# Down projection of a hybrid layer: sums of quarters stored by the gate and up stage, products summed over all pairs in PSUM

## The chip, the cores and the metric

The kernel runs on one core of one Trainium2 chip. The metric is the device time of one execution in microseconds (us). All engines of the core take part: TensorE (PE; PEld is its weight load), VectorE (DVE), ScalarE (ACT), GpSimd (POOL) and the queue of SyncE (SP), which issues nearly all transfers between DRAM and the on-chip memory SBUF. Matmul results are built in PSUM, which has eight banks of 128 x 512 float32.

## The reference

One layer: attention in two head groups, an output projection with a residual, and then the feed-forward part, which is what the change touches. There are 2048 tokens, the model width is 1024, the inner width `D_FF` is 2816, and all is float32.

```python
x = x + jnp.einsum('bse,ed->bsd', mixed, w_o[l])
h = rmsnorm(x, g_ffn[l])
act = jax.nn.silu(jnp.einsum('bsd,df->bsf', h, w_gate[l])) * jnp.einsum('bsd,df->bsf', h, w_up[l])
x = x + jnp.einsum('bsf,fd->bsd', act, w_down[l])
return rmsnorm(x, g_final)
```

## The kernel before

**Precision.** A float32 operand is split into a high part (ScalarE's rounding cast to fp32r) and a low part (the operand less the high part, a subtraction). A product then takes three matmuls: high x high, high x low and low x high. Such a split is therefore one ACT cast and one subtraction, on DVE or on POOL.

**Products of quarters.** Each large matrix product is done by the Strassen-Winograd scheme: both factors are cut into quarters, seven products of sums of quarters take the place of eight, and sums of the products give the result's quarters. In the names, A11, A12, A22 and S1 to S4 are a left quarter or a sum of left quarters; the products in the down projection are P1 to P7. P1 is A11 by its right quarter, P2 A12, P3 S4, P4 A22, P5 S1, P6 S2 and P7 S3, each by a quarter or a sum of quarters of `w_down`.

**Gate and up (`ffn_in`).** The tokens are taken in two halves (`t2`) of 1024. At the start of each half, `operands` loads the normalised input hT and makes the seven left operands with both parts, which stay in SBUF. Then come eleven pairs `j` of 128-wide blocks of the inner width. For each, `quads` runs the seven products with the gate weights (g) and then the seven with the up weights (u), 12 matmuls per product, in the PSUM banks X, Y and Z. `weights` loads the raw weights into a pool `rw` of four buffers (each 512 KB), forms their sums on DVE and splits them. `gated` applies the silu, and `upped` multiplies gate by up (L1094) and stores each of the four quarters of the activation to DRAM (L1097, 256 KB each). The first pair of each half uses `first_quads`, with one bank per product.

**Down (`ffn_out`).** Here the left factor is the activation, the right `w_down`. Each half of the tokens goes through three groups of pairs (4, 4 and 3); within a group the seven products follow in the order P1, P6, P2, P7, P5, P4, P3. A class `Pair` loads a pair's activation and weight quarters into two tiles E and F, and its method `operands` makes, product by product, the sums (L1154 to L1166) in place and the split (`split`: cast L1147, subtraction L1148) into a tile `o4` from a pool of six. The sums and part of the subtractions go to POOL: `alt` is POOL for odd pairs. A product's 12 matmuls per pair are at L1254. The PSUM banks are three sets of four (X, Y and Z, of which two can be in use at once), and after each group every product is evicted: `evict` adds it to the residual x1 held in SBUF (L1205), P1 goes to a tile `a1` (L1201, L1199), which is later added to three quarters (L1212). After the last group `square`, `finish` and the scalings L1192 apply the final normalisation and L1193 stores the result. The last two products of all are run together, one quarter of the tokens after the other.

**Order.** The order of the instructions on each engine is set when the program is built, from the order of the code and the pools' buffers. An engine works through its instructions in that order and waits on semaphores. SP's transfers do the same; each of them also waits for the eighth before it to have landed.

## Time and profile before

| | before |
|---|---|
| time, median of 3 runs | 2446.41 us (2442.75 to 2448.05) |
| the profiled execution, its own time | 2443.37 us |
| its span | 2441.6 us (1.8 us lie around it) |
| busy in the span: PE, DVE, ACT, POOL | 2312.3, 1702.8, 1054.3, 531.5 us |
| mean granted TensorE clock | 0.983 |
| gate and up, first half of the tokens | 1096 to 1526 us |
| gate and up, second half | 1526 to 1964 us |
| down projection | 1964 to 2441.6 us |
| moved by SP's queue in the span | 349.20 MB |

A row of the profile names the line, the engine, the operation, the tile written and the tiles read. A group of rows gives how many there are, their busy time in us, the mean of one in ns, and then the time that the engine stood idle just ahead of them with what ended it ("<-"). In a timeline the idle time and what ended it stand in brackets.

### The profile page before, as it was taken

How to read it: one execution, taken by the hardware profiler on the slowest of the kernel's cores; microseconds unless marked ns; L12 is line 12 of the kernel's file. 1: busy time of each engine (PE TensorE's matmuls, PEld its weight loads, DVE VectorE, ACT ScalarE, POOL GpSimd, SP SyncE). 2: the span in 40 equal slices, each digit the busy share in tenths (PEclk: the TensorE clock that was granted, in tenths of full speed). 3: DMA queues.
4: the chain of work that ended last, by engine and by line, in shares of the span. 5: the costliest groups of instructions: out<-in, count | busy, mean ns of one | idle time of the engine just before them, and what ended most of it. 6: DMA issues, size and time to landing. Idle time of an engine off the chain costs nothing.

```text
span 2441.6 us, 33440 instructions
## 1 busy us (share of the span) xinstructions
PE 2312.3 (95%) x11765; PEld 1949.7 (80%) x11765; DVE 1702.8 (70%) x3239; ACT 1054.3 (43%) x2371; POOL 531.5 (22%) x417
## 2 busy tenths in 40 slices
PE   7999999997999889998999999899999989998997
PEld 7987788886999777776888888688888868876885
DVE  5335554447999877659566665965556468999899
ACT  5323355554898843335333323432333233343333
POOL 2211211111111011113110111311011064345532
PEclk9999999998999999999999999999999999998999
DMA  7656666569987877744222222422222254334221
GB/s 219 213 181 215 166 180 179 151 157 241 230 217 196 230 214 201 249 180 145 82 86 91 78 87 74 138 83 87 77 90 84 100 220 138 138 104 139 102 87 69
DMA packets 245975, 361.17 MB, mean 148 GB/s; under 512 B 19872, under 2 KB 148512, under 8 KB 240304
## 3 DMA queue, kind: packets, MB, share of 16 engines
q1 hardware_dynamic: 242032, 349.20, 47.5%
q0 software_dynamic: 3488, 9.51, 1.3%
q8 instruction: 93, 1.52, 0.3%
q14 instruction: 74, 0.61, 0.1%
q10 hardware_dynamic: 288, 0.33, 0.0%
HBM read 240.36 MB, written 118.62 MB: 147 GB/s over the span
## 4 chain that ended last, share of the span: by engine, by line
PE 43%; DVE 10%; issue 3%; DMA 3%; POOL 2%; ACT 1%; SPq 0%; DVEq 0%; POOLq 0%; ACTq 0%
PE Yu L1022 7%; PE Yg L1022 7%; PE Zu L1022 5%; PE Xu L1022 5%; PE Zg L1022 4%; PE Xg L1022 4%; PE bY L1254 3%; PE acco L885 3%; DVE o L1148 3%; PE bZ L1254 2%; PE bX L1254 1%; DVE xo L1205 1%; DVE xo L1192 1%; DMA E<-in_w_down_dram 1%; DVE F L1161 1%
## 5 line engine op out<-in xcount | busy, mean ns | idle before, releaser
L1094 POOL TENSOR_TENSOR c<-c,c 128x512 f32<-128x512 f32 x66 | 103.2, 1566 | 664.9 <-DVE c L1040 311.6
L987 ACT CAST wh<-T 128x512 fp32r<-128x512 f32 x176 | 108.5, 622 | 252.4 <-PE Yg L1022 76.1
L1254 PE MATMUL bY<-o 128*128 128x512 f32 x792 | 195.5, 403 | 20.8 <-DVE o L1148 9.4
L468 DVE TENSOR_TENSOR hl<-pt,hl 128x512 fp32r<-128x512 f32 (+1 forms) x224 | 145.8, 658 | 80.9 <-ACT hl L467 80.4
L1254 PEld LDWEIGHTS bY<-o 128*128 128x128 f32 x792 | 152.6, 195 | 60.7 <-DVE o L1148 11.9
L443 ACT ACTIVATE p<-t,m 128x256 f32<-128x256 f32 (+1 forms) x384 | 177.4, 480 | 17.8 <-DVE m L668 17.8
L169 PE MATMUL acc<-hh,wh 128*128 128x512 f32 x416 | 170.2, 409 | 0.7 <-DVE vt L239 0.7
L169 PE MATMUL acc<-hh,wl 128*128 128x512 f32 x416 | 170.4, 410 | 0.0
L169 PE MATMUL acc<-hl,wh 128*128 128x512 f32 x416 | 170.1, 409 | 0.0
L885 PE MATMUL acco<-woh,oT 128*128 128x512 f32 x512 | 163.9, 398 | 4.4 <-ACT oT L856 3.4
L486 PE MATMUL o<-hl,v 128*128 128x128 f32 (+1 forms) x816 | 141.9, 294 | 7.5 <-DVE hl L468 6.8
L467 ACT CAST hl<-pt 128x512 fp32r<-128x512 f32 (+1 forms) x224 | 125.1, 568 | 45.3 <-PE pt L462 45.1
L421 PE MATMUL s<-k,q 128*128 128x256 f32 (+1 forms) x768 | 122.1, 290 | 18.2 <-DMA k<-kB 8.5
L462 PE MATMUL pt<-ident,p 128*128 128x128 f32 x848 | 134.3, 280 | 4.1 <-DVE hl L468 1.8
L989 DVE TENSOR_TENSOR wl<-T,wh 128x512 fp32r<-128x512 f32 x176 | 124.5, 712 | 17.0 <-ACT wh L987 16.7
L1254 PE MATMUL bX<-o 128*128 128x512 f32 x528 | 125.4, 393 | 6.7 <-DVE o L1148 4.0
L1254 PEld LDWEIGHTS bX<-o 128*128 128x128 f32 x528 | 98.7, 189 | 31.5 <-DVE o L1148 6.8
L1254 PE MATMUL bZ<-o 128*128 128x512 f32 x528 | 122.7, 389 | 1.1 <-DVE xo L1205 1.1
L421 PEld LDWEIGHTS s<-k,q 128*128 128x128 f32 x768 | 100.8, 192 | 26.3 <-DVE nma L558 7.3
L486 PEld LDWEIGHTS o<-hl,v 128*128 128x128 f32 x816 | 111.5, 193 | 12.7 <-DVE hl L468 10.8
L885 PEld LDWEIGHTS acco<-woh,oT 128*128 128x128 f32 x512 | 97.2, 190 | 26.0 <-ACT oT L856 4.1
L425 DVE CUSTOM_DVE_ANT_0 t<-s,tab 128x256 f32<-128x256 f32 (+1 forms) x344 | 112.9, 369 | 5.7 <-PE s L421 2.7
(467 smaller groups left out, 6125.8 us busy)
## 6 DMA issues: line engine op xcount, KB each, us to landing
wraw_g<-in_w_gate_dram SPq DMA_DIRECT2D x44, 512.0 KB
wraw_u<-in_w_up_dram SPq DMA_DIRECT2D x44, 512.0 KB
actS<-c SPq DMA_DIRECT2D x65, 256.0 KB
k<-kB SPq DMA_DIRECT2D x32, 512.0 KB
E<-actS SPq DMA_DIRECT2D x22, 512.0 KB
E<-in_w_down_dram SPq DMA_DIRECT2D x44, 256.0 KB
F<-actS SPq DMA_DIRECT2D x22, 512.0 KB
F<-in_w_down_dram SPq DMA_DIRECT2D x44, 256.0 KB
```

Of the source, the lines that this page charges most:

```text
L169: nc.tensor.matmul(acc, a[:, k, :], mv, start=(n == 0), stop=(n == 3 * KC - 1))
L421: nc.tensor.matmul(s[:, i, :n], b["q"], b["k"][m], start=(m == 0), stop=(m == 1))
L425: nc.vector.tensor_tensor_reduce(out=b["kv"](t[:, i, :n]), in0=b["kv"](s[:, i, :n]), in1=b["tab"], scale=-0.125, scalar=init, op0=ALU.add, ...
L443: nc.scalar.activation(b["pv"](p[:, i, :n]), b["tv"](b["t"]), AF.Exp, scale=-1.0, bias=nm[:, c:c + 1], accum_out=l[:, c:c + 1])
L462: nc.tensor.transpose(pt[:, sl, :], p[:, i, hfn * P:(hfn + 1) * P], ident)
L467: nc.scalar.copy(hi, pt[:, a:z, :])
L468: nc.vector.tensor_sub(lo, pt[:, a:z, :], hi.bitcast(F32))
L486: nc.tensor.matmul(out, v[:, vi, :], mov, start=(first and n == 1), stop=(last and n == 2 * len(jobs)))
L885: nc.tensor.matmul(acc, oT[kk // 2][:, kk % 2, a, i * P:(i + 1) * P], b[:, kk, :], start=(n == 0), stop=(n == 11))
L989: nc.vector.tensor_sub(lo, src, hi.bitcast(F32))
L1022: nc.tensor.matmul(bank, a[:, k], b[:, k], start=(first and m == 0), stop=(m == 11), skip_group_check=not first)
L1254: nc.tensor.matmul(bank[i], ops[kk][:, u, 0, i * P:(i + 1) * P], ops[kk][:, v, 1, :], start=(n in ("P1", "P6", "P5") and kk == 0 and m == ...
```

## The change

The sums of quarters for the down projection are no longer formed in the down stage.

- In gate and up, `upped` forms the four sums S1 to S4 of activation quarters on POOL (four operations more per pair) and stores seven operands per pair, not four, to a new DRAM array `sc.S`.
- For each pair of the first half of the tokens, a new function `fold_down` loads the pair's two blocks of `w_down` into two of the four `rw` buffers, forms the four sums of weight quarters on DVE, and stores them to a new DRAM array `sc.wT` (two loads and two stores of 512 KB per pair). It stands between the gate products and the up products of the pair.
- For the second half of the tokens, `operands` forms S3 and the low part of A12 on DVE; for the first half they stay on POOL.
- In the down stage, a product is summed over all eleven pairs in its PSUM banks before the next product begins, so there are no groups and each product is evicted once per half. Every operand tile (left and right, 256 KB each) is loaded from DRAM when its product is due, into a pool of fourteen raw tiles; ACT casts it and DVE subtracts, into a pool of eight split tiles. POOL makes no operand. Evictions are put between the next product's pairs (`late`). In the last product of all, P3, the last five pairs are held back and run one quarter of the tokens at a time, each quarter being finished at once.

The number of matmuls is the same.

```diff
+        wdv = w_down[0].rearrange("(k p) n -> p k n", p=P)
+        def fold_down(j):
+            r, q = (rw.tile([P, 2, 512], F32, tag="raw", name="draw") for _ in range(2))
+            for t, f in ((r, 2 * j), (q, 2 * j + 1)):
+                nc.sync.dma_start(t.rearrange("p h n -> p (h n)"), wdv[:, f, :])
+            nc.vector.tensor_sub(r[:, 0], r[:, 1], r[:, 0])
+            nc.vector.tensor_sub(r[:, 1], q[:, 1], r[:, 1])
+            nc.vector.tensor_sub(q[:, 1], q[:, 1], r[:, 0])
+            nc.vector.tensor_sub(q[:, 0], q[:, 0], q[:, 1])
+            nc.sync.dma_start(sc.wT[0:2, :, j, :].rearrange("n p c -> p n c"), r)
+            nc.sync.dma_start(sc.wT[2:4, :, j, :].rearrange("n p c -> p n c"), q)
...
             e = nc.vector if t2 else nc.gpsimd
...
-                nc.gpsimd.tensor_sub(s3, q[0, 0], q[1, 0])
+                e.tensor_sub(s3, q[0, 0], q[1, 0])
                 put("S3", s3)
-                put("A12", q[0, 1], nc.gpsimd)
+                put("A12", q[0, 1], e)
...
                 def upped(a, b, v, psum):
+                    G = nc.gpsimd
                     g = gate[a, b]
-                    (nc.vector if psum else nc.gpsimd).tensor_mul(g, v, g)
-                    q = nc.gpsimd if t2 == NT // 2 - 1 and j == DFF // (2 * P) - 1 else nc.sync
-                    q.dma_start(sc.act[2 * t2 + a, :, 2 * j + b, :], g)
+                    (nc.vector if psum else G).tensor_mul(g, v, g)
+                    act[a, b] = g, v
+                    if (a, b) != (1, 0):
+                        store(f"A{a + 1}{b + 1}", g)
+                    if (a, b) == (1, 0):
+                        (a22, s1), (a11, _) = act[1, 1], act[0, 0]
+                        G.tensor_add(s1, g, a22)
+                        store("S1", s1)
+                        G.tensor_sub(v, s1, a11)
+                        store("S2", v)
+                        G.tensor_sub(g, a11, g)
+                        store("S3", g)
+                    if (a, b) == (0, 1):
+                        G.tensor_sub(v, g, act[1, 0][1])
+                        store("S4", v)
...
+                if t2 == 0:
+                    fold_down(j)
                 quads(S, views[1], j, "u", "v", upped)
...
+        rp, op, xp, cp, sp = (pool(n, b) for n, b in (("r4", 14), ("op4", 8), ("x4", 3), ("c4", 1), ("s4", 2)))
...
+        def operands(t2, n, j):
+            r = rp.tile([P, 2, 512], F32, tag="r", name="r4")
+            nc.sync.dma_start(r[:, 0], sc.S[t2, ORDER.index(n), :, j, :])
+            if n in RIGHT:
+                nc.sync.dma_start(r[:, 1], sc.wT[RIGHT[n], :, j, :])
+            else:
+                f, hf = {"P1": (2 * j, 0), "P2": (2 * j + 1, 0), "P3": (2 * j + 1, 1)}[n]
+                nc.sync.dma_start(r[:, 1], wdv[:, f, hf * 512:(hf + 1) * 512])
+            o = op.tile([P, 2, 2, 512], F32R, tag="o", name="o4")
+            nc.scalar.copy(o[:, 0], r)
+            V.tensor_sub(o[:, 1], r, o[:, 0].bitcast(F32))
+            return o
...
+        late = []
+        for t2 in range(NT // 2):
+            for n in ORDER:
...
+                tail = 5 if n == "P3" and t2 == NT // 2 - 1 else 0
+                held = []
+                for j in range(NP):
+                    o = operands(t2, n, j)
+                    if j < NP - tail:
+                        for i in range(4):
+                            cell(n, banks[t2, BANK[n]], o, j, i)
+                    else:
+                        held.append((o, j))
+                    if late and j != 4:
+                        late.pop(0)()
...
+                for i in range(4):
+                    for o, j in held:
+                        cell(n, banks[t2, BANK[n]], o, j, i)
+                    if held:
+                        evict(t2, n, i)
+                if not held:
+                    late = [lambda i=i, n=n, t2=t2: evict(t2, n, i) for i in range(4)]
+                    c = {"P6": (0, 1), "P2": (1, 1), "P7": (1, 0)}.get(n)
+                    if c:
+                        late += [lambda i=i, c=c, t2=t2: add_first(t2, c, i) for i in range(4)]
```

Three places show how the instructions lie. The first is SP's queue over one pair of the first half of the tokens in gate and up: the weight loads (wraw_g, wraw_u) and the stores of the activation (actS, from the tiles `gate` and c) before.

```order
L996 DMA wraw_g<-in_w_gate_dram 128x4x256
L1097 DMA actS<-gate 128x512
L996 DMA wraw_g<-in_w_gate_dram 128x4x256
L1097 DMA actS<-c_13480 128x512
L996 DMA wraw_u<-in_w_up_dram 128x4x256
L1097 DMA actS<-c_13509 128x512
L1097 DMA actS<-c_13524 128x512
L996 DMA wraw_u<-in_w_up_dram 128x4x256
```

The same place now, with the loads of `w_down` (draw) and the stores of its sums (wT):

```order
L1005 DMA wraw_g<-in_w_gate_dram 128x4x256
L1118 DMA actS<-c_14165 128x512
L1096 DMA draw<-in_w_down_dram 128x1024
L1118 DMA actS<-c_14319 128x512
L1118 DMA actS<-c_14209 128x512
L1118 DMA actS<-c_14349 128x512
L1118 DMA actS<-c_14194 128x512
L1118 DMA actS<-c_14370 128x512
L1096 DMA draw<-in_w_down_dram 128x1024
L1101 DMA wT<-draw 128x2x512
L1005 DMA wraw_u<-in_w_up_dram 128x4x256
L1102 DMA wT<-draw 128x2x512
```

The second load of `w_down` and the up weights now stand behind the stores of all sums, and a store of a weight sum stands between the two up loads. The weight loads of a pair are issued during the pair before it, in both programs.

The second place is DVE at the beginning of the down stage, ahead of and in the second product, P6 (o is a split tile, E, F and ST a pair's raw quarters and sums), before:

```order
L1157 TENSOR_TENSOR ST<-F,E 128x1024
L1148 TENSOR_TENSOR o_18850<-ST,o_18850 128x1024
L1157 TENSOR_TENSOR ST<-F,E 128x1024
L1148 TENSOR_TENSOR o_18867<-ST,o_18867 128x1024
L1148 TENSOR_TENSOR o_18884<-ST,o_18884 128x1024
L1148 TENSOR_TENSOR o_18901<-ST,o_18901 128x1024
L1148 TENSOR_TENSOR o_18920<-F,o_18920 128x1024
L1161 TENSOR_TENSOR F<-F,ST 128x2x512
```

Now, from the twenty-first tile on, at the end of the second product (r is a raw tile, L1220 the addition of P1 to a quarter of the residual xo, L1211 an eviction):

```order
L1178 TENSOR_TENSOR o_19414<-r_19411,o_19414 128x1024
L1178 TENSOR_TENSOR o_19432<-r_19429,o_19432 128x1024
L1220 TENSOR_TENSOR xo_19092<-xo_19092,a_19033 128x512 x8
L1178 TENSOR_TENSOR o_19450<-r_19447,o_19450 128x1024
L1178 TENSOR_TENSOR o_19469<-r_19466,o_19469 128x1024
L1211 TENSOR_TENSOR xo_19094<-bY,xo_19094 128x512
L1178 TENSOR_TENSOR o_19488<-r_19485,o_19488 128x1024
L1211 TENSOR_TENSOR xo_19094<-bY,xo_19094 128x512
L1220 TENSOR_TENSOR xo_19094<-xo_19094,a_19033 128x512
```

The sums are gone and each tile has one subtraction; the eight additions of P1 stand together behind the twenty-second tile's, and the first eviction of P6 stands behind the twenty-fourth's, two tiles past the end of that product. The third place is TensorE at the same stage's start, before:

```order
L1254 MATMUL bX<-o_18823 128x512 x12
L1254 MATMUL bY<-o_18850 128x512 x12
L1254 MATMUL bY<-o_18867 128x512 x12
L1254 MATMUL bY<-o_18884 128x512 x12
L1254 MATMUL bY<-o_18901 128x512 x4
L1254 MATMUL bX<-o_18920 128x512 x4
L1254 MATMUL bY<-o_18901 128x512 x8
```

Now:

```order
L1225 MATMUL bX<-o_19190 128x512 x12
L1225 MATMUL bX<-o_19208 128x512 x12
L1225 MATMUL bX<-o_19226 128x512 x12
L1225 MATMUL bY<-o_19248 128x512 x12
L1225 MATMUL bY<-o_19267 128x512 x12
```

The bank set now changes after eleven tiles, not after four.

More of the change, by code (lines that the diff above doesn't have):

```diff
@@ L78, in shape_constants @@
     return {"rope": rope, "mask_a": mask_a, "onehot": oh, "sel": sel}
+ORDER = ("P1", "P6", "P2", "P7", "P5", "P4", "P3")
+LEFT = {n: i for i, n in enumerate(("A11", "S2", "A12", "S3", "S1", "A22", "S4"))}
+RIGHT = {"P5": 0, "P7": 1, "P4": 2, "P6": 3}
 class Scratch:
@@ L1084, in ffn_in @@
             for j in range(DFF // (2 * P)):
-                gate = {}
+                gate, act = {}, {}
                 def gated(a, b, v, psum):
@@ L1202, in evict @@
                 return
-            a, hf = TO[n]
-            d = xs[t2, a][:, i, hf * 512:(hf + 1) * 512]
+            d = quarter(t2, *TO[n], i)
             V.tensor_add(d, src, d)
-            if not end:
-                return
-            add_a1 = {"P6": (0, 1, G), "P2": (1, 1, V), "P7": (1, 0, V)}.get(n)
-            if add_a1:
-                c, u, e = add_a1
-                d = xs[t2, c][:, i, u * 512:(u + 1) * 512]
-                e.tensor_add(d, d, a1[t2][:, i])
             if n in ("P2", "P5", "P4", "P3"):
-                square(t2, a, hf, i)
+                square(t2, *TO[n], i)
@@ L1215, in evict @@
             if n in ("P4", "P3"):
-                finish(t2, a, i)
-        steps = [(t2, g, n) for t2 in range(NT // 2) for g in range(len(GROUPS)) for n in ORDER]
-        pairs = {(t2, g): [Pair(t2, j) for j in GROUPS[g]] for t2 in range(NT // 2) for g in range(len(GROUPS))}
-        for p in pairs[0, 0]:
-            p.load(0)
-        for p in pairs[0, 0]:
-            p.load(1)
-        load_x1(0, 1)
-        load_x1(0, 0)
-        bcast_row(nc, gfin, g_final)
-        made = [p.operands("P1") for p in pairs[0, 0]]
@@ new lines, in evict, with add_first, cell @@
+                finish(t2, TO[n][0], i)
+        def add_first(t2, c, i):
+            d = quarter(t2, *c, i)
+            V.tensor_add(d, d, a1[t2][:, i])
+        def cell(n, bank, o, j, i):
+            first = n in ("P1", "P6", "P5")
+            for m, (u, v) in enumerate(((0, 0), (0, 1), (1, 0))):
+                nc.tensor.matmul(bank[i], o[:, u, 0, i * P:(i + 1) * P], o[:, v, 1, :], start=(first and j == 0 and m == 0),
+                                 stop=(j == NP - 1 and m == 2), skip_group_check=not first)
@@ new lines, in ffn_out @@
+        late = []
+        for t2 in range(NT // 2):
+            for n in ORDER:
+                if n == "P1":
+                    a1[t2] = cp.tile([P, 4, 512], F32, tag="a1", name=f"a1{t2}")
+                if n in ("P1", "P6", "P5"):
+                    banks[t2, BANK[n]] = [ps.tile([P, 512], F32, tag="mm", name="b" + BANK[n]) for _ in range(4)]
+                tail = 5 if n == "P3" and t2 == NT // 2 - 1 else 0
[9 more added lines that the diff above has]
+                        late.pop(0)()
+                    if n == "P1" and j == 2:
+                        if t2 == 0:
+                            load_x1(0, 1)
+                            load_x1(0, 0)
+                            bcast_row(nc, gfin, g_final)
+                        else:
+                            load_x1(t2, 1)
+                    if n == "P7" and j == 0 and t2 + 1 < NT // 2:
+                        load_x1(t2 + 1, 0)
+                for i in range(4):
[8 more added lines that the diff above has]
+                        late += [lambda i=i, c=c, t2=t2: add_first(t2, c, i) for i in range(4)]
```

123 lines of the change are left out of this document (15 added, 108 removed).

## The prediction

> **What bounds the kernel now.** I read the busy times by stage first (stretch in us, its length, then busy time and instructions of PE, PEld, DVE, ACT and POOL, then granted clock, DMA share and GB/s). The first six stretches are gate and up for the first and second half of the tokens, each with its start set apart; the last two are the down projection.
>
> ```profile
> 1096.00:1138.00 42.00, 32.57 (x120) 23.93 (x119) 38.41 (x45) 26.72 (x48) 19.64 (x12) 0.88 0.49 168
> 1138.00:1156.00 18.00, 18.00 (x81) 14.91 (x80) 18.00 (x30) 6.23 (x12) 1.29 (x1) 1.00 0.42 136
> 1156.00:1526.00 370.00, 370.00 (x1634) 306.36 (x1633) 225.96 (x320) 117.82 (x200) 47.00 (x31) 1.00 0.25 83
> 1526.00:1566.00 40.00, 32.03 (x119) 22.14 (x117) 38.56 (x43) 19.23 (x35) 21.74 (x13) 0.96 0.47 149
> 1566.00:1590.00 24.00, 23.90 (x106) 19.74 (x106) 23.41 (x39) 8.91 (x16) 3.42 (x1) 1.00 0.33 103
> 1590.00:1964.00 374.00, 373.21 (x1647) 308.68 (x1646) 212.18 (x308) 114.87 (x192) 48.52 (x33) 1.00 0.29 96
> 1964.00:2000.00 36.00, 26.79 (x98) 19.65 (x97) 24.14 (x15) 10.90 (x14) 31.35 (x16) 0.91 0.65 257
> 2000.00:2442.00 442.00, 409.69 (x1754) 330.52 (x1752) 411.85 (x417) 168.63 (x210) 181.32 (x86) 0.97 0.31 107
> ```
>
> Gate and up is TensorE from end to end: 370.00 of 370 and 373.21 of 374 us, with DVE at 61% and 57%. The down projection is not: DVE is busy 411.85 of 442 us there, so TensorE can be held by it. The groups by line in the down projection (1964 to 2442 us) give the matmuls with what they waited for, and DVE's and ACT's main work:
>
> ```profile
> L1254 PE MATMUL bY<-o 128*128 128x512 f32 x792 | 195.5, 403 | 20.8 <-DVE o L1148 9.4 <-ACT o L1147 6.6 <-DVE xo L1205 4.8
> ...
> L1254 PE MATMUL bX<-o 128*128 128x512 f32 x528 | 125.4, 393 | 6.7 <-DVE o L1148 4.0 <-DVE a L1199 2.8
> L1254 PE MATMUL bZ<-o 128*128 128x512 f32 x528 | 122.7, 389 | 1.1 <-DVE xo L1205 1.1
> L1148 DVE TENSOR_TENSOR o<-E,o 128x1024 fp32r<-128x1024 f32 x66 | 99.3, 1528 | 0.7 <-ACT o L1147 0.7
> ...
> L1147 ACT CAST o<-F 128x1024 fp32r<-128x1024 f32 x66 | 67.5, 1050 | 56.9 <-PE bZ L1254 25.0 <-PE bY L1254 23.7 <-DVE o L1148 8.3
> ...
> L1205 DVE TENSOR_TENSOR xo<-bY,xo 128x512 f32<-128x512 f32 x72 | 46.8, 679 | 4.4 <-PE bY L1254 4.4
> ...
> L1192 DVE SCALAR_TENSOR_TENSOR xo<-xo,rs_z,gfin 128x512 f32<-128x512 f32 x32 | 29.0, 954 | 0.7 <-POOL rs_z L110 0.7
> ```
>
> Waits are 20.8 + 6.7 + 1.1 = 28.6 us, all on the making of operands or on evictions. What the stage loses in all is read from TensorE's timeline (start, length, what, idle time before it):
>
> ```profile
> 1964.09 1.07 PE L1254 MATMUL bX<-o 128*128 128x512 f32 x4
> 1966.24 3.01 PE L1254 MATMUL bX<-o 128*128 128x512 f32 x12 [1.08 <-DVE o L1148]
> ...
> 1978.56 1.19 PE L1254 MATMUL bY<-o 128*128 128x512 f32 x4 [1.20 <-ACT o L1147]
> ...
> 1986.42 7.28 PE L1254 MATMUL bY<-o 128*128 128x512 f32 x24 [3.40 <-ACT o L1147]
> ...
> 2011.04 11.04 PE L1254 MATMUL bY<-o 128*128 128x512 f32 x48
> 2021.92 8.32 PE L1254 MATMUL bZ<-o 128*128 128x512 f32 x36
> ...
> 2216.98 10.50 PE L1254 MATMUL bY<-o 128*128 128x512 f32 x35 [4.71 <-DVE o L1148]
> ...
> 2240.39 1.57 PE L1254 MATMUL bY<-o 128*128 128x512 f32 x5 [1.71 <-DVE o L1148]
> ...
> 2424.81 4.24 PE L1254 MATMUL bZ<-o 128*128 128x512 f32 x18
> ```
>
> Between 2011.04 and 2021.92 lie 48 matmuls without a gap: 0.2267 us each, so 2.72 us for the 12 of one operand tile, and 792 + 528 + 528 = 1848 matmuls take 418.9 us at best. They run from 1964.09 to 2424.81 + 4.24 = 2429.05, which is 465.0 us: **46.0 us are lost**, and from 2429.05 to the span's end at 2441.6 lies a **tail of 12.5 us**. The stage is 418.9 + 46.0 + 12.5 = 477.5 us. Of the loss, 14.3 us fall before 2011.04 (46.95 us; the groups up to there, four of them shown, hold 144 matmuls that need 32.65), where each group's first operands are late; the clock granted there is 0.91, so part of it is slow matmuls behind the gaps. The waits of 4.71 and 1.71 us stand at the change from one group of pairs to the next.
>
> Why operands are late stands on DVE and POOL, which share the making of them:
>
> ```profile
> 1998.01 6.71 POOL L1148 TENSOR_TENSOR o<-F,o 128x1024 fp32r<-128x1024 f32 x2
> 2002.39 3.41 DVE L1148 TENSOR_TENSOR o<-F,o 128x1024 fp32r<-128x1024 f32 x1
> ...
> 2011.53 1.21 DVE L1148 TENSOR_TENSOR o<-E,o 128x1024 fp32r<-128x1024 f32 x1
> ```
>
> The same subtraction takes DVE 3.41 us while POOL runs one and 1.21 us alone. More than the sums themselves, it is POOL's share of them that makes DVE late.
>
> **The change part by part. Down projection.** Removed are all sums (DVE's and POOL's), POOL's share of the splits, and two of three evictions per product. Each of the 154 operand tiles (2 halves of the tokens x 7 products x 11 pairs) now costs DVE one split at 1.21 us (L1178 of the new kernel) and ACT one cast at 1.05, against 2.72 us of TensorE. DVE's whole stage: 154 x 1.21 = 186 us, 48 evictions at 0.68 = 33, 24 additions of the first product at 0.68 = 16, 32 final scalings at 0.95 = 30, some 10 of small operations: 275 us of about 420. POOL has only 16 small operations there, so the 3.41 us case is gone. TensorE's order is tile after tile, with eight split tiles and fourteen raw ones in front of it, and its PSUM sets change every 11 tiles (30 us). What is left to lose:
>
> - The start. The first split still stands on DVE behind the last addition of the up stage, as the one that gave 1.08 us at 1966.24 does now. POOL's sums of the last pair run into the first ten microseconds and can stretch three splits to 3.4 us, 0.7 us over a tile's matmuls each. 1.1 + 2.1 is about **3 us**; ends 1 (POOL is done earlier) and 6 (a granted clock of 0.91 over 36 us adds 3).
> - The middle. Evictions wait on DVE for a product's last matmul and hold the splits behind them, with two tiles (5.4 us) already split; the eight additions to the residual stand in one row (8 x 0.68 = 5.5 us) behind tile 21, with up to eight tiles split. Neither should empty the buffer: **2 us**; ends 0 and 10 (each of the 13 product changes at 0.8).
> - The tail. Now:
>
> ```profile
> 2435.49 2.73 DVE L1192 SCALAR_TENSOR_TENSOR xo<-xo,rs_z,gfin 128x512 f32<-128x512 f32 x4
> 2430.55 8.04 SPq L1193 DMA_DIRECT2D out_dram<-xo  x10
> ```
>
>   The last scaling ends 2438.2, the last store is issued by 2438.6 and the span ends 3.0 us later. Two quarters are finished per step, so four scalings stand in a row. In the new kernel only product P3 is left, one quarter of the tokens at a time: after the last matmul come an eviction 0.7, square and row sums about 1.5, POOL's power 0.9, two scalings 1.4, hand-overs about 1, and the store 3.4: **9 us**; ends 8 and 11.
>
> Sum: 418.9 + 3 + 2 + 9 = **433 us against 477.5, a gain of 44.5**; ends 428 and 446.
>
> **Gate and up.** Here every microsecond of TensorE is taken, so a gain can only come at the two starts. A pair lasts 14 products x 2.72 = 38.1 us, of which DVE is busy 23.3 (61%) and POOL 4.8. Added per pair: four POOL sums, in the first half also four DVE subtractions, two loads and two stores of 512 KB, and three more stores of 256 KB. The prices:
>
> ```profile
> L1094 POOL TENSOR_TENSOR c<-c,c 128x512 f32<-128x512 f32 x66 | 103.2, 1566 | 664.9 <-DVE c L1040 311.6
> 1547.46 1.75 POOL L966 TENSOR_TENSOR A12l<-hraw,A12h 128x512 fp32r<-128x512 f32 x1
> 1547.98 1.78 DVE L966 TENSOR_TENSOR S1l<-s,S1h 128x512 fp32r<-128x512 f32 x1
> ...
> 1557.04 0.68 DVE L966 TENSOR_TENSOR S4l<-s,S4h 128x512 fp32r<-128x512 f32 x1
> ```
>
> POOL: 4.8 + 4 x 1.57 = 11 of 38 us. DVE: four subtractions at 0.68 are 2.7, and each POOL sum can stretch one DVE operation from 0.68 to 1.78, 4.4 in all: 30.4 of 38.1 us (80%), still under TensorE. The cover is that slack of 7.7 us and weights that are loaded a whole pair ahead; without it a pair would cost what DVE runs over. Behind the new waits on SP's queue (seven stores that wait for POOL, two for DVE's subtractions) stand the weight loads, and for them DVE and then TensorE; the last sum is done some 26.5 us after a pair's up products begin (the sixth product ends at 16.3, its eviction takes 0.7, and six POOL operations of 1.57 follow), and the weights loaded behind it are wanted a pair later. I take **0** per pair, with 1 us as the other end, so 0 to 10 over ten pairs.
>
> The starts are another matter, since DVE has no slack there (38.41 of 42, then 18.00 of 18, and 38.56 of 40 us). In the first half the four subtractions of the first pair (2.7 us) and its 1 MB of loads come before the up weights, which now get their buffers some 3 to 7 us later: **+3.5**, ends 0 and +6. In the second half S3 and the low part of A12 go from POOL to DVE, eight operations at 0.68 = 5.4 us; but POOL then keeps only one operation in three, and each of those it loses gave back up to 1.1 us to DVE (8 x 1.1 = 8.8). The reloading of hT stands behind the sums' stores of the last pair. **+1**, ends -2 and +4.
>
> **Feeding it.** All operands now come from DRAM: 154 x 2 x 256 KB = 80.7 MB, with 8.4 MB of x1, 8.4 of output and 0.5 of the gain some 98 MB in 430 us, 228 GB/s, against a mean of 119 now. The DMA view of the stage, in 40 slices of 12 us:
>
> ```profile
> DMA  7920378000097300077002749640003260000035
> GB/s 263 398 111 0 123 274 308 1 0 1 1 310 255 139 1 0 0 251 266 12 23 88 240 177 319 220 167 1 0 1 116 86 238 1 1 0 0 2 132 219
> ...
> actS<-c POOLq DMA_DIRECT2D x2, 256.0 KB, 3.5
> ```
>
> The same rows of 2 KB moved at 398 GB/s in a slice with DMA 90% busy; a tile every 2.72 us asks 193. One transfer took 3.5 us, and up to eight of SP's may be open (each waits for the eighth before it), so 8 x 262 KB / 3.5 us is far above the need. I cost it at 0; its other end is the slower case below.
>
> **Sum.** -44.5 + 3.5 + 1 = **-40**. The profiled execution took 2443.4 us, which becomes 2403; it lies 3 us under the median of the runs shown, 2446.4, so in those terms **2406**. Ends: -49.5 - 2 = -51.5 and -31.5 + 6 + 4 + 10 = -11.5, each with all unknowns to one side.
>
> **The rivals.** *Gate and up pays for the sums.* Any delay per pair of the first half counts ten times: at 3 us it is 30, and the time 2436; only above 4 us per pair does the whole become slower. For it: the fold's tiles take two of the four raw buffers, so weights are loaded two thirds of a pair ahead instead of a whole one. Against it: DVE's 7.7 us of slack and TensorE's 370.00 of 370 now.
>
> *The down projection keeps half its losses.* Splits, evictions and additions share one DVE queue in order. If the middle still loses 20 us, because the two tiles of lead are gone at each product's end, 13 x 1.5, the gain is 26.5 and the time 2424. For it: 8.7 us of today's waits are on evictions (4.8 + 2.8 + 1.1). Against it: DVE falls from 93% to about 65%.
>
> *The queue starves TensorE (slower).* The loads are 308 transfers of 256 KB, all issued by SP in order, with x1's loads and the first half's output stores among them. They decide from 468 / 308 = 1.52 us per transfer, that is when fewer than 2.3 are under way at 3.5 us each. With two under way the stage takes 308 x 1.75 = 539 us and the tail of 9, 70 more than now: 2517. For it: a store that waits for DVE stops every load behind it. Against it: the slices at 263 and 398 GB/s (one 256 KB in 0.66 us) and fourteen raw buffers. The Trainium skill, "DMA: Bandwidth & Descriptors", section "Anatomy of one DMA", gives about 2.0 us fixed per transfer plus its bytes at 436 GB/s: an estimate by that page is 2.6 us for 256 KB, and one after another 801 us for the stage, a time near 2780. The slice at 398 GB/s says that here such times overlap.
>
> **How the numbers follow.** The forecast 0.68 (its own range 2397 to 2418), gate and up 0.12, half the losses 0.12, starved 0.06, others 0.02. A measurement of this kernel tells about 0.2% (5 us) from no change. Faster: 0.68 + 0.12 + 0.07 of the gate and up case + 0.01 = 0.88; the same 0.03; slower 0.06 + 0.03 = 0.09. The range goes from the low end, 2395, to 2432, which takes in the second rival and most of the first.
>
> **What would show it.** Right: the down stage's DVE at about 65% with splits near 1.2 us, waits of TensorE on operands under 6 us in all, a tail near 9, DMA near 230 GB/s throughout, TensorE still at 100% between the starts of gate and up. Wrong: waits on L1178 or on DMA in the down stage; TensorE under 98% in the first half of gate and up with waits on the split weights.

## The result and the profile after

The changed kernel takes **2404.39 us** (median of 4 runs, 2402.85 to 2406.46) against 2445.3 us before (4 runs, the three shown and one beside them): a ratio of **0.9833, 95% interval 0.9816 to 0.985**. The forecast was 2406 in a range of 2395 to 2432. The profiled execution has a span of 2402.7 us, 38.9 less than before.

The busy times by stage, cut where the stages of the changed kernel lie (columns as in the prediction):

```profile
1099.00:1210.00 111.00, 101.10 (x401) 79.34 (x401) 97.28 (x124) 45.45 (x81) 39.32 (x25) 0.92 0.54 184
1210.00:1530.00 320.00, 319.65 (x1411) 264.35 (x1410) 231.98 (x311) 98.81 (x173) 91.56 (x58) 1.00 0.47 157
1530.00:1590.00 60.00, 50.72 (x197) 36.75 (x196) 54.29 (x75) 26.93 (x47) 17.97 (x11) 0.94 0.42 136
1590.00:1974.00 384.00, 383.22 (x1691) 316.95 (x1690) 252.59 (x324) 117.83 (x197) 117.55 (x74) 1.00 0.31 102
1974.00:2010.00 36.00, 34.90 (x154) 28.54 (x154) 27.61 (x20) 19.94 (x22) 11.76 (x11) 1.00 1.03 387
2010.00:2403.00 393.00, 385.20 (x1700) 318.63 (x1698) 230.24 (x271) 163.55 (x203) 12.41 (x16) 0.99 0.63 214
```

In the down stage DVE is busy 27.61 + 230.24 = 258 of 428 us (60%), against 436 of 478 before, and TensorE runs through. Its timeline there, first two rows and last, with the groups by line:

```profile
1974.74 1.07 PE L1225 MATMUL bX<-o 128*128 128x512 f32 x4
1976.91 29.33 PE L1225 MATMUL bX<-o 128*128 128x512 f32 x128 [1.10 <-DVE o L1178]
...
2389.83 5.38 PE L1225 MATMUL bZ<-o 128*128 128x512 f32 x23
```

```profile
L1178 DVE TENSOR_TENSOR o<-r,o 128x1024 fp32r<-128x1024 f32 x154 | 191.2, 1252 | 131.9 <-ACT o L1177 124.1 <-DMA r<-actS 3.0 <-DMA r<-wT 3.0
L1225 PE MATMUL bY<-o 128*128 128x512 f32 x792 | 180.5, 389 | 0.0
...
L1225 PE MATMUL bX<-o 128*128 128x512 f32 x528 | 120.6, 389 | 1.1 <-DVE o L1178 1.1
L1225 PE MATMUL bZ<-o 128*128 128x512 f32 x528 | 120.3, 389 | 0.0
```

One wait of 1.1 us is left of 28.6. The 1848 matmuls run from 1974.74 to 2395.2, 420.5 us, and the tail is 7.5. The stage is **428.0 us against 477.5**. A split costs DVE 1.25 us on average, where before the means were 1.45 (operands from F), 1.53 (E) and 1.99 (ST). The first eleven, with POOL's last sums beside them, take 17.2 us back to back, 1.56 each:

```profile
1975.55 17.20 DVE L1178 TENSOR_TENSOR o<-r,o 128x1024 fp32r<-128x1024 f32 x11
```

What gate and up pays is read between three marks: the first matmul of FA in either half of the tokens and the first bX. For the kernel before and the changed one (the first bX of either is quoted already):

```profile
1096.90 0.79 PE L1060 MATMUL FA<-A11h,wh 128*128 128x512 f32 x1 [0.34 <-ACT A11h L965]
...
1522.32 0.39 PE L1060 MATMUL FA<-A11h,wh 128*128 128x512 f32 x1
```

```profile
1099.54 0.80 PE L1069 MATMUL FA<-A11h,wh 128*128 128x512 f32 x1 [0.34 <-ACT A11h L974]
...
1530.89 0.39 PE L1069 MATMUL FA<-A11h,wh 128*128 128x512 f32 x1
```

Before: 425.4 and 441.8 us; now: 431.4 and 443.9. So gate and up gives back 8.0 of the 49.5 us that the down stage gains. The first FA itself is 2.6 us later although nothing ahead of it changed: over all profiles of this study it lies between 1096.9 and 1109.2, and the clock granted between 540 and 610 us differs (third figure from the end). The rows of before and of x3, the earliest and the latest (0.90 and 0.71; some 8 of the 12 us between them arise about there):

```profile
540.00:610.00 70.00, 55.03 (x379) 48.54 (x378) 53.15 (x256) 33.32 (x117) 12.52 (x21) 0.90 0.90 225
```

```profile
540.00:610.00 70.00, 57.04 (x300) 50.87 (x298) 43.36 (x216) 23.25 (x78) 13.84 (x23) 0.71 0.95 228
```

The changed kernel has 0.90 there as well, so its 2.6 us come from elsewhere. The stages are therefore compared between marks below, from one profile of each kernel. Where their code is the same, they repeat to about 1 us either way: the first half of before's code took 425.4, 426.6 and 427.7 in three kernels that share it (mean 426.6), of the changed one 431.4, 431.7 and 431.8 (431.6); the second half 441.8, 442.7 and 442.9 (442.5), and 443.9, 443.9 and 444.2 (444.0). By these means the cost is 5.0 + 1.5 = 6.5 us. Each ratio in the table is to runs of the kernel before in the same session; x1, x2 and x3 leave work out, as said below.

| kernel | first half | second half | down | sum | ratio to before, 95% |
|---|---|---|---|---|---|
| before | 425.4 | 441.8 | 477.5 | 1344.7 | 1 |
| changed | 431.4 | 443.9 | 428.0 | 1303.2 | 0.9833 (0.9816 to 0.985) |
| no fold (x1) | 426.6 | 444.2 | 428.2 | 1299.0 | 0.9833 (0.9805 to 0.9861) |
| no POOL sums (x2) | 428.1 | 438.1 | 428.0 | 1294.2 | 0.9795 (0.9772 to 0.9818) |
| before, POOL's part out (x3) | 427.7 | 442.7 | 433.6 | 1304.0 | 0.984 (0.9807 to 0.9872) |
| folds in pairs 2 to 9, then 3 to 5 (x4) | 429.8 | 449.0 | 427.9 | 1306.7 | 0.9857 (0.9836 to 0.9878) |
| S3, A12 back on POOL (x5) | 431.8 | 447.1 | 428.0 | 1306.9 | 0.9851 (0.9825 to 0.9877) |
| four buffers in v (x6) | 433.1 | 447.0 | 427.9 | 1308.0 | 0.9841 (0.9821 to 0.9861) |
| before, POOL's part on DVE (x7) | 426.6 | 442.9 | 445.5 | 1314.9 | 0.9875 (0.985 to 0.9901) |
| folds in pairs 4 to 11, then 7 to 9 (x8) | 425.5 | 449.9 | 428.0 | 1303.3 | 0.9824 (0.9805 to 0.9844) |
| four raw tiles (x9) | 431.7 | 443.9 | 439.3 | 1314.9 | one run, no ratio |
| sums on DVE (x11) | 432.6 | 437.9 | 431.8 | 1302.3 | 0.9839 (0.9816 to 0.9862) |
| no POOL in gate and up (x12) | 430.0 | 437.5 | 431.7 | 1299.2 | 0.983 (0.9802 to 0.9858) |
| x13, put together from these | 425.4 | 435.6 | 428.0 | 1288.9 | **0.9776 (0.9751 to 0.9801)** |

### The profile page after: what moved, and what is told of

It reads as the page before. It is cut to its first block, busy times and chain, and to the rows that moved or that the text cites. A ratio compares the mean times of both kernels' runs of the same rounds, so it can differ in the third digit from the quotient of the medians.

```text
span 2402.7 us, 33903 instructions
## 1 busy us (share of the span) xinstructions
PE 2300.4 (96%) x11765; PEld 1947.0 (81%) x11765; DVE 1604.5 (67%) x3151; ACT 1054.1 (44%) x2371; POOL 468.1 (19%) x418
## 4 chain that ended last, share of the span: by engine, by line
PE 51%; DVE 5%; DMA 4%; issue 1%; POOL 0%; ACT 0%; SPq 0%; DVEq 0%; POOLq 0%; ACTq 0%
PE bY L1225 7%; PE Yu L1031 7%; PE Yg L1031 6%; PE bZ L1225 5%; PE bX L1225 5%; PE Xu L1031 4%; PE Zu L1031 4%; PE Zg L1031 4%; PE Xg L1031 4%; PE acco L893 3%; DMA ob<-oB 1%; DVE wl L998 1%; DMA draw<-in_w_down_dram 1%; DVE xs L915 1%; DMA hraw<-hT 0%
## 5 line engine op out<-in xcount | busy, mean ns | idle before, releaser
L1178 DVE TENSOR_TENSOR o<-r,o 128x1024 fp32r<-128x1024 f32 x154 | 191.2, 1252 | 131.9 <-ACT o L1177 124.1
L1177 ACT CAST o<-r 128x1024 fp32r<-128x1024 f32 x154 | 162.2, 1054 | 225.0 <-DMA r<-in_w_down_dram 50.8
L1225 PE MATMUL bY<-o 128*128 128x512 f32 x792 | 180.5, 389 | 0.0
L998 DVE TENSOR_TENSOR wl<-T,wh 128x512 fp32r<-128x512 f32 x176 | 153.2, 882 | 0.3
```

The costliest lines, as they stand in the source:

```text
L998: nc.vector.tensor_sub(lo, src, hi.bitcast(F32))
L1177: nc.scalar.copy(o[:, 0], r)
L1178: V.tensor_sub(o[:, 1], r, o[:, 0].bitcast(F32))
L1225: nc.tensor.matmul(bank[i], o[:, u, 0, i * P:(i + 1) * P], o[:, v, 1, :], start=(first and j == 0 and m == 0), stop=(j == NP - 1 and m == ...
```

## The experiments

### Why were operands late in the down stage? (x3, x7)

My reason was POOL: its operations are long and stretch DVE's. The rival was the structure, that is groups of four pairs with an eviction after each. Both experiments keep that structure. In x3 POOL's part is left out:

```diff
-                    self.alt.tensor_sub(two(self.E, 1, 3), two(self.E, 0, 2), two(self.E, 1, 3))
+                    if self.alt is V:
+                        V.tensor_sub(two(self.E, 1, 3), two(self.E, 0, 2), two(self.E, 1, 3))
...
-                    o = self.split(two(self.F, 0, 2), self.alt)
+                    o = self.split(two(self.F, 0, 2), V)
...
-                    G.tensor_sub(self.E[:, 2], self.F[:, 3], self.E[:, 2])
...
-                    G.tensor_add(self.E[:, 0], self.E[:, 0], self.ST[:, 0])
```

> The kernel before, with POOL's part of the down stage's operands left out: POOL's sums are not done (for odd pairs E, F and ST stay unsummed, and the additions of a1 by POOL are left out), and the ten splits that POOL did go to DVE. The groups of four pairs and the evictions after each group stay. By rows of before DVE then has about 154 x 1.21 + 55 x 1.21 + 120 x 0.68 + 70 = 405 us of work at most, against 412 busy now. Theory (POOL's operations, which stretch a split from 1.21 to 3.4 us, make the operands late): the 46 us that the down stage loses shrink to 20 or less, the stage from 477.5 to about 450, the time to about 2418. Rival (the groups and their evictions in DVE's order make them late): the loss stays above 35 us and the time above 2434.

In x7 nothing is left out, all of it is DVE's:

```diff
-    V, G = nc.vector, nc.gpsimd
+    V, G = nc.vector, nc.vector
```

> The kernel before with all that POOL did for the down stage's operands moved to DVE, nothing left out. In the run without POOL's part DVE was busy 364 us of the stage and the stage took 433.6; the sums that were left out there are 20 of 128x1024 at 1.14 and 52 of 128x512 at 0.61, 55 us: 419 us of DVE for 419 us of matmuls. Theory (operands come late because POOL's operations are long and stretch DVE's): DVE does all the work at its unstretched times and is just as busy as TensorE, the stage takes 440 to 455 us against 477.5 and the whole 20 to 35 us less than before. Rival (it is the amount of work beside TensorE that costs, wherever it is done): the stage stays at 470 or more.

The down stage as one stretch, before, x3, x7 and changed, one row from each kernel's profile:

```profile
1964.00:2442.00 478.00, 436.48 (x1850) 350.17 (x1848) 435.99 (x431) 179.53 (x223) 212.67 (x101) 0.97 0.34 119
```

```profile
1979.00:2413.00 434.00, 420.86 (x1852) 346.84 (x1850) 364.30 (x441) 183.16 (x224) 20.93 (x20) 0.99 0.37 131
```

```profile
1967.00:2412.00 445.00, 423.64 (x1849) 346.84 (x1847) 414.62 (x513) 181.44 (x223) 23.10 (x19) 0.99 0.36 128
```

```profile
1974.00:2403.00 429.00, 420.10 (x1852) 347.17 (x1851) 257.84 (x291) 183.49 (x224) 24.16 (x27) 0.99 0.66 228
```

x3 falls to 433.6 us, further than I had expected of it (450): of 46 us lost, 4.1 remain beside a tail of 10.6. TensorE's waits in it:

```profile
PE bX L1258 <- DVE o L1148: 1.4, 2, 1.1
PE bY L1258 <- ACT o L1147: 1.2, 1, 1.2
```

x7 shows that it is not the amount of work. With every sum on DVE the stage takes 445.5 us, 32.0 less than before, by moving work from an engine that had time to one that had none. DVE runs 82 instructions more (513 against 431) in less busy time (414.6 us against 436.0), because hardly any of its operations meets one of POOL's, which has 19 operations there and not 101. Of the 17.5 us that are left to 428, the longer tail is 5 and TensorE's waits take 8 more (9.1 against 1.1); what the other 4 are is not shown. Of the waits listed, 6.3 of 9.0 are on DVE, which is now nearly as busy as TensorE (414.6 and 423.6 us), and the rest on ACT's casts:

```profile
PE bY L1254 <- DVE o L1148: 3.6, 4, 2.2
PE bY L1254 <- ACT o L1147: 1.7, 1, 1.7
PE bX L1254 <- DVE o L1148: 1.4, 2, 1.1
PE bY L1254 <- DVE xo L1205: 1.3, 2, 0.7
PE bX L1254 <- ACT o L1147: 1.0, 1, 1.0
```

So the groups and their evictions cost 4 us at most once POOL's part is out. The Trainium skill, "SBUF — State Buffer", section "SBUF: two separate sides", says that POOL and a DVE operation with two SBUF inputs take a shared pair of ports in turn, each for a whole instruction; 3.41 us against 1.21 in the prediction's rows, and these two runs, agree. The evictions, which read one input from PSUM, were not stretched: 679 ns before (L1205 in the prediction) and 685 now.

### Does the queue keep up? (x9)

```diff
-("r4", 14)
+("r4", 4)
```

> The changed kernel with four raw tiles in the down stage's pool, not fourteen. With the changed kernel the stage's loads run at about 400 GB/s in its first 95 us, while the fourteen buffers and the eight split ones are filled, and at 193, TensorE's pace, where they are full. Theory (the supply is twice the need, and each tile waits little): with four buffers, 2 MB, the stage stays within 2 us of 428. Rival (the depth covers the queue's order, stores and x1 loads among the loads): TensorE waits on operands at x1's loads and at the output stores of the first half, 10 us or more in all, and the stage takes 438 or more.

The DMA view of the changed kernel's down stage (40 slices of 10.7 us):

```profile
DMA  9999999956665656689988475476565666100513
GB/s 349 399 397 413 405 386 386 340 178 207 189 192 193 194 194 195 196 271 327 380 276 311 150 238 191 161 221 189 190 191 193 195 195 194 50 1 11 188 50 147
DMA packets 49200, 97.96 MB, mean 228 GB/s; under 512 B 5504, under 2 KB 5504, under 8 KB 48661
```

At first the loads run at 340 to 413 GB/s, until the buffers are full, and then at TensorE's 193. With four buffers TensorE waits once:

```profile
PE bX L1225 <- ACT o L1177: 8.4, 1, 8.4
```

My expectation of this single run was wrong and the rival's figure right: the stage is 11.3 us longer. But the wait stands between 1986 and 1994 us of that run, within the first product, behind whose third pair the two loads of x1 (2 MB each) are issued. The output stores cause none. What the wait of 8.4 us does not explain are for the most part slower matmuls behind it: the clock granted from 1986 to 2010 us was 0.79, against 1.00 in the changed kernel. The queue is fast enough everywhere but around x1's loads, and there the depth covers it.

### What does gate and up pay? (x1, x2)

x1 has no folds, x2 no sums on POOL:

```diff
-                if t2 == 0:
-                    fold_down(j)
```

> The changed kernel with the sums of w_down left out: no loads, subtractions and stores of fold_down; the four products that used them read a plain quarter of w_down instead, so the down stage moves the same bytes. Theory: the changed kernel's gate and up stage is 8.0 us longer than before (from the first matmul of FA to the start of the down stage), and 5.3 of it, the stretch from the first FA matmul to the up products of the third pair (109.7 us against 104.5), come from the first two pairs' eight subtractions on a DVE that has no slack there. Then this stretch is back at about 104.5 and the time near 2398.5. Rival (POOL's sums stretch DVE's operations and cause it): the stretch stays at 108 or more and the time above 2402. Down stage unchanged by either, 428 us.

```diff
-                        G.tensor_add(s1, g, a22)
...
-                        G.tensor_sub(v, s1, a11)
...
-                        G.tensor_sub(g, a11, g)
...
-                        G.tensor_sub(v, g, act[1, 0][1])
```

> The changed kernel with POOL's four sums S1 to S4 of the activation left out (the quarters are stored in their places, so stores and bytes stay). Theory: the sums cost the start of the second half of the tokens 2.1 us, where DVE's S3 waits for a buffer of the v pool that POOL's chain holds (3.0 us wait of TensorE on S3h), and the first pairs' waits on u, up to 1.5 us; the stretch from FA to the third pair's up products stays at 108 to 110. Time 2401 to 2402.5. Rival (POOL's sums are what costs in the first half, by holding DVE): that stretch falls below 106, and the time to 2398 or less.

First half: sums alone cost nothing (x1: 426.6, the mean of before), folds alone 1.5 us (x2: 428.1), both together 5.0. Between the first up products of one pair and the next, folds add 1.35 us ahead of the second pair's, with the sums or without; 2.5 us ahead of the third pair's, and 0.65 later, appear only where both are there. The stretch that the two expectations speak of, from the first FA to the third pair's up products, took 109.8 us in the changed kernel, 105.6 in x1 (its theory had 104.5) and 107.1 in x2 (between its theory's 108 and its rival's 106).

In the changed kernel DVE stands back to back from 1124 to 1158 us (but for 0.12 us), and in this stretch lie the subtractions of two pairs' folds, eight of them; first and last:

```profile
1129.35 0.68 DVE L1097 TENSOR_TENSOR draw<-draw 128x512 f32<-128x512 f32 x1
...
1157.81 0.68 DVE L1100 TENSOR_TENSOR draw<-draw 128x512 f32<-128x512 f32 x1
```

Besides a wait that x1 has as well, TensorE waits for DVE once there, and twice more after POOL's first sums, which begin at 1166 us:

```profile
1139.11 0.50 PE L1031 MATMUL Yu<-S2h,wl 128*128 128x512 f32 x1 [0.97 <-DVE wl L998]
...
1185.92 0.50 PE L1031 MATMUL Yu<-S3h,wh 128*128 128x512 f32 x1 [0.63 <-DVE u L1043]
...
1206.39 0.50 PE L1031 MATMUL Yg<-S3h,wh 128*128 128x512 f32 x1 [0.89 <-DVE u L1043]
```

Second half: here it is the sums that cost, 5.8 us (443.98 to 438.15), as the rival in x2's expectation had it for the first half. I had expected 2.1, and up to 1.5 more at the first pairs. In the whole times x2 shows it (2395.65 us, where I had 2401 or more); x1's median, 2404.1, does not lie under the changed kernel's, and its interval reaches 7 us to either side of that one's ratio: its 5 us are seen between the marks alone.

### The start of the second half (x5, x6)

```diff
-            e = nc.vector if t2 else nc.gpsimd
+            e = nc.gpsimd
```

> The changed kernel with S3 and the low part of A12 made by POOL in both halves of the tokens, as in the kernel before. By the profiles, gate and up of the second half (from its first FA matmul to the start of the down stage) took 441.8 us before, 443.9 in the changed kernel and 438.2 where POOL's sums were left out. Theory: the move to DVE gains about 3.6 us (441.8 to 438.2) because POOL's operations stretch DVE's, and the sums cost 5.7; undone, the second half takes about 447.5 and the whole 3 to 4 us more than the changed kernel. Rival (as the prediction priced the move, eight operations more on a full DVE): undone, the second half falls to 441 or less. The first half, 431.4, and the down stage, 428, stay.

Undone, the second half takes 447.1 us, as the theory had it (447.5): moving eight operations *to* the fuller engine had gained 3.1.

```diff
-            ("t3", 6), ("a3", 1), ("g3", 6), ("v3", 3), ("whl3", 9), ("u3", 5)))
+            ("t3", 6), ("a3", 1), ("g3", 6), ("v3", 4), ("whl3", 9), ("u3", 5)))
```

> The changed kernel with four buffers in the pool v of gate and up, not three. At the start of the second half DVE's S3 subtraction waits 1.2 us for POOL's second sum, since S3's tile takes a buffer of v that the last pair's sums hold, and TensorE then waits 3.0 us for S3's high part. Theory (a buffer wait): the 3.0 us wait goes, the second half falls from 443.9 to 441 or 442. Rival (DVE is full there, stretched by POOL, and any wait is made up behind it): within 1 us of 443.9, the wait only moves to a later operand.

In the changed kernel DVE and TensorE wait at this place:

```profile
1548.44 1.73 DVE L985 TENSOR_TENSOR s<-hraw 128x512 f32<-128x512 f32 x1 [1.16 <-POOL c L1133]
```

```profile
1550.87 0.80 PE L1069 MATMUL FS<-S3h,wh 128*128 128x512 f32 x1 [3.03 <-ACT S3h L974]
```

With a fourth buffer in x6 this wait is gone, and others stand in its place:

```profile
1563.21 0.50 PE L1069 MATMUL FA<-A22h,wh 128*128 128x512 f32 x1 [2.70 <-ACT A22h L974]
1567.34 0.50 PE L1069 MATMUL FA<-A11h,wh 128*128 128x512 f32 x1 [1.02 <-ACT A11h L974]
1576.10 0.80 PE L1069 MATMUL FA<-A22l,wh 128*128 128x512 f32 x1 [5.24 <-POOL A22l L975]
```

447.0 against 443.9: neither range holds. As the rival had it, the wait only moves, and the stage is 3 us longer besides. The extra buffer also changes the order of the work (TensorE's products at this start come in another order), so the run does not test the buffer alone; it shows that the named wait's going does not by itself shorten the stage.

### Where can the folds stand? (x4, x8)

```diff
-                if t2 == 0:
-                    fold_down(j)
+                if t2 == 0 and 1 <= j <= 8:
+                    fold_down(j - 1)
+                if t2 == 1 and 2 <= j <= 4:
+                    fold_down(j + 6)
```

> The changed kernel with fold_down moved away from the start: the eleven folds stand in the second to ninth pair of the first half and the third to fifth pair of the second half, one per pair, so that the first pair and the boundary have none. Theory: a fold costs nothing where TensorE bounds and DVE has slack, so the 5.3 us of the start come back but for the second pair's share (up to 2): 2399 to 2401. Rival (each fold costs its share of DVE or of SP's queue wherever it stands): 2403 to 2406.

x8 differs in the pairs: `j >= 3` of the first half and `6 <= j <= 8` of the second.

> The changed kernel with the folds in the fourth to eleventh pair of the first half (eight) and the seventh to ninth of the second (three). In the profile of the changed kernel TensorE waits 0.35 us in the first half behind its third pair, and with the fold left out the first half took 426.6 us against 431.4. Theory (a fold costs only while DVE is still catching up with a half's start): the first half takes 427 to 428.5, the second 444 to 445, and the whole is 3 to 4 us less than the changed kernel. Rival (the folds' buffers make the weight loads late wherever they stand, as in the run with folds in the third to fifth pair of the second half, 449.0 against 443.9): the second half takes 447 or more and nothing is gained.

In x8 the eight folds of the first half cost nothing (425.5, every pair 38.08 us from the third on), but the three of the second cost 6, and in x4 they cost 5. So x8's theory holds for the first half and its rival for the second; x4 took 2410.87 us, longer than both of its ranges. In both, DVE's late sums u hold TensorE in pairs near the folds; x8's two largest waits:

```profile
1791.78 0.50 PE L1031 MATMUL Yg<-S3h,wh 128*128 128x512 f32 x1 [0.77 <-DVE u L1043]
...
1832.01 0.50 PE L1031 MATMUL Yg<-S3h,wh 128*128 128x512 f32 x1 [1.85 <-DVE u L1043]
```

In x4 the chain ahead of its wait can be followed on DVE: it idles for a weight load, and then come operations stretched by POOL's, the fold's subtraction (L1097) among them, ahead of u.

```profile
1634.61 0.69 DVE L1013 TENSOR_TENSOR T<-wraw_g,T 128x512 f32<-128x512 f32 x1 [4.14 <-DMA wraw_g<-in_w_gate_dram]
...
1639.83 1.78 DVE L998 TENSOR_TENSOR wl<-T,wh 128x512 fp32r<-128x512 f32 x1
1641.53 1.77 DVE L1097 TENSOR_TENSOR draw<-draw 128x512 f32<-128x512 f32 x1
1643.22 1.75 DVE L1021 TENSOR_TENSOR T<-wraw_g,T 128x512 f32<-128x512 f32 x1
1644.89 0.68 DVE L1043 TENSOR_TENSOR u<-Yg,c 128x512 f32<-128x512 f32 x1
```

x8 has the same chain ahead of its wait of 1.85 us. The late load is not the folds' doing: in the changed kernel DVE idles 4.1 to 5.7 us for it in each pair of the second half from 1631 us on, without a fold, and TensorE waits for nothing. From the start of that load's first sum (L1013) to the end of u DVE takes 9.3 to 9.4 us there, 11.0 us with the fold's subtraction in between (x4, x8), and 7.9 to 8.6 us in x13 below, with a fold but without POOL. So by these times what makes u late is the fold's subtraction among operations that POOL stretches; no run takes out one of the two alone. In the first half of x8 DVE idles only 1.2 to 2.8 us for this load; why stays open.

### POOL out of gate and up (x11, x12), and all together (x13)

x11 puts `upped`'s operations on DVE; x12 also those of `operands`:

```diff
-                    G = nc.gpsimd
+                    G = nc.vector
```

> The changed kernel with the four sums S1 to S4 and the three products of gate and up that POOL makes put on DVE, so that POOL has no work per pair. Seven operations at 0.68 are 4.8 us of DVE per pair, while POOL's seven of 1.57 to 1.7 stretch DVE's by up to 1.1 each, 7.7. Theory (as in the down stage, POOL's help costs DVE more than the work itself): the first half falls from 431.4 to 430 or less, the second from 443.9 to 441 or less, the whole to 2400 or less. Rival (DVE is full at the starts and what is added there delays TensorE): the first half takes 433 or more, the second 446 or more.

```diff
-            e = nc.vector if t2 else nc.gpsimd
+            e = nc.vector
...
-                put("A22", q[1, 1], nc.gpsimd)
+                put("A22", q[1, 1], e)
```

> As the run before, and S3 and the low parts of A12 and A22 made by DVE in both halves too: POOL does nothing in gate and up. At a half's start twelve operations on POOL become 8.2 us of DVE in the first half, and four, 2.7 us, in the second. Theory (each of them stretched a DVE operation by up to 1.1 us, and POOL makes them late): the first half takes as long as in the run before or up to 3 us less, the second up to 2 us less. Rival (DVE is full there): the first half takes 4 us or more longer than in the run before.

The second half gains 6.1 and 6.5 us. The first does not gain in x11 (432.6, between the two ranges expected), and 1.6 in x12. The down stage loses 3.8, which x11's expectation left out; the whole takes 2408.14 us, not the 2400 or less expected. The sums of the last pair now stand ahead of the stage's first split on DVE, and TensorE waits 3.3 us, as x12 shows:

```profile
1975.95 0.69 DVE L1138 TENSOR_TENSOR c<-c,c 128x512 f32<-128x512 f32 x1
1976.56 9.17 DVE L1178 TENSOR_TENSOR o<-r,o 128x1024 fp32r<-128x1024 f32 x8
```

```profile
1977.83 7.55 PE L1225 MATMUL bX<-o 128*128 128x512 f32 x25 [3.27 <-DVE o L1178]
```

x13 takes from each what it showed: no POOL but for that last pair, folds in the fourth to eleventh pair and in the last three of the second half.

```diff
-            e = nc.vector if t2 else nc.gpsimd
+            e = nc.vector
...
-                put("A22", q[1, 1], nc.gpsimd)
+                put("A22", q[1, 1], e)
...
-                    G = nc.gpsimd
+                    G = nc.gpsimd if t2 and j == DFF // (2 * P) - 1 else nc.vector
...
-                if t2 == 0:
-                    fold_down(j)
+                if j >= (8 if t2 else 3):
+                    fold_down(j if t2 else j - 3)
```

> The changed kernel with gate and up's sums, products and splits on DVE (POOL keeps only the sums of the very last pair, which otherwise stand ahead of the down stage's first split and cost 3.3 us there), and the folds in the fourth to eleventh pair of the first half and the last three of the second. From the profiles: folds in the fourth to eleventh pair cost nothing (first half 425.4 us), no POOL work gives the second half 437.5, the down stage with the last sums on POOL takes 428. Theory: first half 425 to 427, second half 437.5 to 440, down 428, together 1291 to 1295 us from the first FA matmul against 1303.2 in the changed kernel and 1344.7 before: a ratio to before near 0.979. Rival (three folds in the second half cost 2 us each again, as in the seventh to ninth pair): the second half takes 443 or more, the whole 1297 or more, and the ratio stays within the changed kernel's interval, at 0.982 or more.

The first half is back at before's 425.4, the second is 435.6, 6 us under before's: with the sums and folds in it, gate and up is no longer than before. What the kernel before would gain with POOL out of gate and up was not run, so what sums and folds cost by themselves here is not shown. **2392.31 us (median of 5 runs, 2391.35 to 2398.01), ratio 0.9776 (0.9751 to 0.9801)**, under the interval of the changed kernel. Two stretches of gate and up where TensorE is busy throughout, in the changed kernel and in x13, show what DVE gains:

```profile
1210.00:1520.00 310.00, 309.65 (x1366) 256.08 (x1365) 226.81 (x303) 94.74 (x166) 91.56 (x58) 1.00 0.47 160
1590.00:1960.00 370.00, 370.00 (x1634) 306.36 (x1633) 248.69 (x319) 114.36 (x193) 114.16 (x70) 1.00 0.31 101
```

```profile
1210.00:1520.00 310.00, 310.00 (x1370) 256.76 (x1369) 221.57 (x356) 96.59 (x165) 0.00 (x0) 1.00 0.48 158
1590.00:1960.00 370.00, 370.00 (x1634) 306.39 (x1633) 246.89 (x387) 113.08 (x190) 2.52 (x4) 1.00 0.38 123
```

DVE runs 121 operations more than in the changed kernel, and its busy time falls from 475.5 to 468.5 us. TensorE gains only 0.35 us in these stretches; the other 14 us of gate and up lie outside of them, nearly all at the starts of the halves.

## Why the prediction was right

| term | forecast | measured |
|---|---|---|
| down: lost at the start | 3 | 1.1 |
| down: lost in the middle | 2 | under 1 |
| down: tail | 9 | 7.5 |
| down, change | -44.5 | -49.5 |
| first half of gate and up | +3.5 | +5.9 (by the means: +5.0) |
| per pair between the starts | 0 | 0, but for 0.65 in one, counted above |
| second half | +1 | +2.1 (by the means: +1.5) |
| sum | -40 | -41.5 |

The measured column goes by the marks of the two profiles. The sum came so near by luck: the down stage gained 5.0 us more than forecast and gate and up paid 3.5 more. Step by step:

- **What bounds.** "It is POOL's share of them that makes DVE late" was the central claim, and x3 and x7 bear it out on the old structure: 44 of the 49.5 us come when POOL's part is left out, 32 when it is only moved.
- **The down stage's terms.** All three were set too high. I charged 2.1 us for splits that POOL's last sums stretch at the start. DVE's first eleven splits did take 1.56 us each, but that is less than the 2.72 us of a tile's matmuls, and only the wait of 1.1 us remained. The tail had hand-overs of about 1 us too many. The evictions, feared to empty the buffer, never did. DVE was forecast at 65% and is at 60%. The DMA rate of 230 GB/s "throughout" holds only as a mean: 340 to 413 GB/s for 85 us, then about 193.
- **The start of the first half** is the term that was mis-sized. "The four subtractions of the first pair" should have been those of two pairs, since DVE's back-to-back stretch reaches to 1158 us. But the mechanism that I priced, the folds by themselves, costs only 1.5 us (x2); that they and POOL's sums cost more together than apart was not in the sum at all.
- **The start of the second half** was right only as a sum: the move to DVE gained 3.1 (x5) to 4.4 (x2 against before) where 3.4 was priced, and the sums cost 5.8 where the +1 leaves 4.4 for all the rest. S3's tile behind POOL's chain, in the pool v, was not foreseen.
- **A reading.** The waits of 4.71 and 1.71 us do not stand at a change of groups, as the prediction says. They stand in the second and the fourth product (P6 and P7) of the first group of the second half, whose operands are sums that POOL helps to make, which fits the central claim.
- **The rivals.** A steady cost per pair: no, every pair but one takes 38.08 us from the third on. Half the losses stay: no. A starved TensorE: at first the loads ran at twice the need. The estimate of one transfer after another at 2.6 us rests on the Trainium skill, "DMA: Bandwidth & Descriptors", section "Anatomy of one DMA — SWDGE (gpsimd) path", whose fit is for single transfers issued by the GpSimd queue. These are SP's, with up to eight under way: in the second slice of 10.7 us, at 399 GB/s, 256 KB came every 0.66 us. x9 shows what would have made it partly true: fewer buffers at x1's loads.

## What to carry to other kernels

An idle POOL is not free help for a full DVE: price a move to POOL by what its operations add to DVE's, and try the move back before anything larger. Here that one line (x7) gives 29.8 of the 41.5 us. Work put at a place where one engine runs back to back can cost its full time there (two folds' subtractions are 5.4 us, and 5.0 were lost, though only 1.5 without POOL's sums); the same work a few pairs later can cost nothing. And a wait that the profile names is shown to be a cause only when its removal shortens the stage, which x6's did not.

## What was not expected

- Moving all of POOL's operand work onto a DVE that was busy 91% of the stage made the stage 32 us shorter and DVE less busy (436.0 to 414.6 us with 82 operations more).
- The stage ahead of the change varied by 12 us between profiles of identical instructions, with a granted clock of 0.90 in one and 0.71 in another between 540 and 610 us. With 4 or 5 runs of a version, whole times could not separate versions that differ by 4 us (x1's interval); stage marks of one profile each could, to about 1 us either way.
